# A seven-product form for half of the output projection, spread between HGRN2's last projection tiles, with the residual in four tiles

## The chip, the cores and the metric

The kernel runs on one core of a Trainium2 chip. Its engines work side by side, each on its own queue of instructions: PE (TensorE) multiplies matrices, DVE (VectorE), ACT (ScalarE) and POOL (GpSimd) do elementwise work, and SP issues most of the DMA transfers. The metric is the device time of one execution in microseconds; before the change it is 1578.18 us, the median of three runs.

## The reference, cut to what matters

The block works on 512 tokens of width 1024 in float32: a SwiGLU feed-forward part (FFN1), two token mixers side by side (HGRN2 and Mamba-2), a merge of the two, a second feed-forward part (FFN2), a gate with per-layer embeddings and a last norm. The change lies at the merge:

```
gate_a, gate_b = jnp.split(jax.nn.sigmoid(br_gates), 2, axis=-1)
mixed = gate_a * (o_hg @ w_hg_out[l]) + gate_b * (y @ w_ssm_out[l])
h = h + mixed @ w_out[l]
h = h + 0.5 * swiglu(rms_norm(h, ffn2_norm[l]), ffn2_w13[l], ffn2_w2[l])
```

`w_hg_out` and `w_out` are 1024 x 1024, so `mixed @ w_out` has 512 tokens, an inner dimension of 1024 and 1024 outputs. All products are wanted at float32 accuracy.

## The kernel before

**Three matmuls for one product.** Every operand of a large product is kept as two tiles, a rounded part (hi) and the rest (lo). `split` (L529) makes them: ACT casts (L530), DVE subtracts (L531). `mm` (L515) then issues three matmuls, hi x hi, hi x lo, lo x hi (L518 to L520), into one PSUM bank.

**Units and look-ahead.** The whole kernel is a list of `Unit`s. A unit has weight pieces (`Half`, cut from a `Chunk`) and a function that issues its matmuls. `run` (L388) goes through the list in order. Ahead of each unit it loads and splits weight pieces of later units, as far as the unit's look-ahead numbers allow (`AHEAD`..., L40 to L43) and as `room` (L141) says that enough blocks stay free. After each stretch of matmuls a `slot` lets background work (norms, transposes) advance by a step. What is issued `aside` may be placed elsewhere in its engine's queue by the scheduler behind it, which orders each engine's queue by a modelled timeline when the program is built.

**Memory.** `Arena` holds two blocks of eight units of 1 KB per partition and 46 blocks of four units (`BLOCKS`, L36). `find` (L83) takes the place of least cost: a freed place costs 130 less the number of frees since then, down to 0; tiles of up to four units pay 99 more in a block of eight (L95). `room` counts the empty blocks of four only. A tile of 1024 float32 columns is four units, one whole small block. The residual h (`Tokens`, L284) is two tiles of eight units, with two token tiles of 1024 columns in each; no other tile in the program is that large.

**Seven products.** In both FFNs the matrix products are done two blocks by two in the Strassen-Winograd way, with seven products of half-sized blocks for eight. The order is `ORDER = (1, 2, 6, 5, 7, 3, 4)` (L850), and the names of each product's operands are in `PRODUCTS`: quarters of the weights a, b, d and sums S1 to S4; quarters of the activations e, g, h and sums T1 to T4. A weight chunk of this kind loads five raw pieces, three of which get a second quarter added by a DMA from POOL's queue (`load`, L472); S2 and S4 are summed on DVE (L503, L506). `HiddenQ` (L253) makes the activation operands. The function `down` inside `ffn` (L758) runs the seven products of the FFN's second matrix: each product is 2 x 2 calls of `mm` with 512 columns, and its bank is added straight into two quarters of h by DVE (L780). `_merge` (L1387) spreads two lists of units evenly over one another.

**The stretch around the change.** Gate tiles first; then the eight tiles of `w_hg_out`, each 24 matmuls of 128x512 (`tile`, L659). When tile d is through, `ho_done` (L1526) multiplies its bank with the gate, adds the Mamba-2 share and splits the result: block d of the mixed activations. `mix_end` (L1537) then allocates h, reads it back from DRAM, loads FFN2's norm gain and allocates FFN2's activation operands. `wide` (L824) runs the output projection, one half of the output columns at a time, four token tiles each, 24 matmuls a tile; in the first half the last two inner blocks come in a second pass (`LATE`). `wout_done` (L1567) adds each bank to h on DVE (L1569). After the second half of a token tile its norm starts (`norm_gen`, L572): a square on ACT, a power on POOL, a scaling on DVE (L569), then PE transposes (L208), copies on ACT (L211) and splits. FFN2's first unit `first` (L716) begins with the columns of tokens 0 and 1, 96 matmuls of 128x256, and goes on with those of tokens 2 and 3.

Of the kernel before, what the change touches and what calls it, by code (L numbers as in the profile page):

```python
# [48 lines left out]
FFN_PACE, GATE_PACE = 1, 1.75  # L49
# [3 lines left out]
GATES_FIRST, LATE = 12, 2  # L53
# [10 lines left out]
def _cols(c):  # L64
    return slice(c * P, (c + 1) * P)


class Arena:
# [88 lines left out]
    def free(self, *aps):  # L157
        for ap in aps:
            _, st, lo, k = self.live.pop(id(ap))
            self.clock += 1  # L160
            for i in range(lo, lo + k):
                st[i] = self.clock
# [121 lines left out]
class Tokens:  # L284


    def __init__(self, b):
        self.b = b
        self.half = [b.t(2, D) for _ in range(2)]
        self.c = [self.half[c // 2][:, c % 2, :] for c in range(NC)]  # L290

    def __getitem__(self, c):
        return self.c[c]

    def free(self):
        self.b.fr(*self.half)


class Half:
# [47 lines left out]
class Block:  # L347
# [359 lines left out]
    def ffn(self, h, n, w13, w2, done, then=None):  # L707

        U = self.units
        start = len(U)  # L710
        f0s = [sum(PARTS[:k]) for k in range(len(PARTS) + 1)]
        N = len(PARTS)
        hid = [HiddenQ(self) for _ in PARTS[:-1]] + [Hidden(self, PARTS[-1])]
        v = self.nc.vector
# [40 lines left out]
            v.scalar_tensor_tensor(hd, bank, 0.5, hd, ALU.mult, ALU.add)  # L755
            self.frb(bank)

        def down(k):  # L758


            acc = {}
            ch = Chunk(w2, f0s[k] * P, 4, 0, 2 * 512, "w")

            where = {1: ("A", 1), 2: ("C", 1), 6: ("A", 0), 5: ("B", 1), 7: ("A", 0), 3: ("B", 0), 4: ("A", 0)}
            target = {1: (0, 0), 2: (0, 0), 6: (0, 1), 5: (1, 1), 7: (1, 1), 3: (0, 1), 4: (1, 0)}

            def product(wt, p):
                x, fresh = where[p][0], where[p][1] == 1
                op = hid[k].op.pop(PRODUCTS[p][1])
                ds, th = target[p]  # L770
                if fresh:
                    acc[x] = [self.bank() for _ in range(2)]
                for m in range(2):
                    bank = acc[x][m]
                    for j in range(2):
                        self.mm(bank, tuple(y[:, j, _cols(m)] for y in op), (wt[0][:, j], wt[1][:, j]),
                                fresh and j == 0, j == 1, not fresh)
                    hd = h[0][2 * th + m][:, ds * 512:ds * 512 + 512]
                    with self.aside():
                        v.scalar_tensor_tensor(hd, bank, -0.5 if ds else 0.5, hd, ALU.mult, ALU.add)  # L780
                self.fr(*op)
                if p in (2, 3, 4):
                    self.frb(*acc[x])
                yield FFN_PACE
            return [Unit([next(x for x in ch.halves if x.j == PRODUCTS[p][0])], lambda wt, p=p: product(wt, p)) for p in ORDER]

        def last(*wt, t):

            q = len(wt) // 2
# [20 lines left out]
        for k, size in enumerate(PARTS):  # L810
            x = [u for i in range(0, size, 2) for u in gate_up(k, i)]
            if k:
                U += x[:2] + _merge(x[2:], down(k - 1))
            else:
                U += x
        U.append(Unit([], n_end))
# [3 lines left out]
        U.append(Unit([], lambda: freed(hid[-1])))  # L820
        for u in U[start:]:
            u.ahead = AHEAD_FFN

    def wide(self, act, w, done, late=0):  # L824

# [23 lines left out]
PRODUCTS = {1: ("a", "e"), 2: ("b", "g"), 3: ("S4", "h"), 4: ("d", "T4"), 5: ("S1", "T1"), 6: ("S2", "T2"), 7: ("S3", "T3")}  # L849
ORDER = (1, 2, 6, 5, 7, 3, 4)  # L850


class Seven:
# [8 lines left out]
    def product(self, wt, p, pace):  # L862
        b, st = self.b, self.st
        where = {1: "A", 6: "A", 7: "A", 4: "A", 5: "B", 3: "B", 2: "C"}[p]
        fresh = p in (1, 2, 5)
        if fresh:
            st[where] = b.bank()
        bank = st[where].rearrange("p (j t) -> p j t", j=2)
        wh, wl = wt
        for j in range(2):  # L870
            for k in range(4):
                b.mm(bank[:, j], (wh[:, k, _cols(j)], wl[:, k, _cols(j)]), self.n[0].opk(PRODUCTS[p][1], k),
                     fresh and j == 0 and k == 0, k == 3, j == 1 or not fresh)
        with b.aside():
            self.take(p, bank)
        yield pace
# [529 lines left out]
def _plan(b):  # L1406
    nc, ins = b.nc, b.i
    xr = ins["x"].rearrange("(c p) d -> p c d", p=P)
    hv = b.dram.tile([T, D], F32, name="hscr").rearrange("(c p) d -> p c d", p=P)
    pjv = b.dram.tile([T, D], F32, name="proj").rearrange("(c p) d -> p c d", p=P)  # L1410
    outv = b.out.rearrange("(c p) d -> p c d", p=P)
    U = b.units
    h, n1, n2, n3, n4, mixed, oT = [], [], [], [], [], [], []
# [85 lines left out]
    a, o = hg.plan(1), ssd.plan_out(3)  # L1499
    while a or o:  # L1500
        U.extend(a[:3] + o[:1])
        a, o = a[3:], o[1:]
# [9 lines left out]
    s_, acc = {}, {}  # L1512
# [11 lines left out]
        b.fr(x)  # L1524

    def ho_done(d, bank):  # L1526
        if not mixed:
            mixed.append(Act(b, 0, 1))
            mixed[0].k = [None] * KD
        nc.vector.tensor_tensor(s_[d], s_[d], bank, ALU.mult)  # L1530
        nc.vector.tensor_tensor(s_[d], s_[d], acc[d], ALU.add)
        x = mixed[0].k[d] = b.pair(T)
        mixed[0].blocks.append(x)
        b.split(s_[d], *x)
        b.fr(acc[d], s_[d])

    def mix_end():  # L1537
        oT[0].free()
        h.append(Tokens(b))
        for c in range(NC):  # L1540
            nc.sync.dma_start(h[0][c], hv[:, c, :])
        gains["ffn2"] = b.gain_tile(ins["ffn2_norm"])
        n3.append(ActW(b))
        yield 1
# [6 lines left out]
    gates0 = len(U)  # L1551
    U.append(Unit([], lambda: begin("oT", hg_wait)))
    for w, off, act, done in (("w_in", OFF_GA, n2, ga_done), ("w_in", OFF_GB, n2, gb_done), ("w_hg_out", 0, oT, ho_done)):
        for d in range(0, KD, 2):
            n0 = len(U)
            U.extend(b.tiles(Chunk(ins[w], 0, KD, off + d * P, 256, "c"), act,
                             lambda j, bank, d=d, done=done: done(d + j, bank), GATE_PACE))
            if act is oT and d == 0:
                U[n0].need = ["oT"]
        if done is gb_done:  # L1560
            U.append(Unit([], n2_end))

# [4 lines left out]
    def wout_done(t, dh, acc):  # L1567
        dc = slice(dh * 512, (dh + 1) * 512)
        nc.vector.tensor_tensor(h[0][t][:, dc], h[0][t][:, dc], acc, ALU.add)  # L1569
        if dh == 1:  # L1570
            b.start(("n3", t), b.norm_gen(h[0][t], gains["ffn2"], n3[0], t, wait=1, after=(
                lambda: b.fr(gains["ffn2"])) if t == NC - 1 else None))
            if t == NC - 1:
                mixed[0].free()
    b.wide(mixed, ins["w_out"], wout_done, LATE)


    def done2(t):
# [53 lines left out]
```

## Time and profile before

| what | before |
|---|---|
| median of three runs (lowest to highest) | 1578.18 us (1575.81 to 1579.27) |
| the profiled execution, its span | 1577.02 us, 1575.3 us |
| PE busy | 1537.3 us (98%) |
| DVE busy | 1081.1 us (69%) |
| ACT busy | 754.5 us (48%) |
| POOL busy | 173.3 us (11%) |
| mean DMA rate | 143 GB/s |

The span runs from the first to the last instruction of the profiled execution. A PE that is busy is not a PE at its peak, since neighbouring matmuls overlap and their ends are modelled: the distance between starts says how fast they go.

### The profile page before, as it was taken

The page shows a single profiled execution, that of the slowest core. Times are in us where ns is not written, and L with a number is a line of the kernel's source. Part 1 is how long each engine was busy: PE and PEld are TensorE (multiplying, and loading weights), DVE is VectorE, ACT ScalarE, POOL GpSimd, SP SyncE. Part 2 cuts the span into 40 slices and gives each one's busy share as a digit, 9 for nine tenths or more (in the row PEclk, how much of TensorE's full clock was granted, in tenths as well). Part 3 has the DMA queues.
Part 4 walks back from the last instruction along what each step waited for, and adds up shares of the span by engine and source line. Part 5 has one row for each costly group of instructions (what it writes and reads, how often), then busy time and mean ns, then how long its engine had stood idle before and what let it go on. Part 6 is the DMA issues. An engine that isn't in the chain of part 4 may idle for free.

```text
span 1575.3 us, 22345 instructions
## 1 busy us (share of the span) xinstructions
PE 1537.3 (98%) x8894; PEld 1339.3 (85%) x8894; DVE 1081.1 (69%) x1379; ACT 754.5 (48%) x1093; POOL 173.3 (11%) x230
## 2 busy tenths in 40 slices
PE   8999999999998999999999999999999999999997
PEld 7989999988886887878888788888889999999986
DVE  7789888775568675867646654434348987897853
ACT  6555554554456445452454455433136654545542
POOL 2101101000012010110012011100002011001000
PEclk9999999999999999999999999999999999999999
DMA  9967867565233254364431522342239768676521
GB/s 298 213 160 189 214 147 192 123 208 161 67 95 108 88 167 141 120 182 141 121 100 61 174 69 72 107 134 94 94 90 236 171 175 206 148 193 148 200 68 54
DMA packets 216012, 225.52 MB, mean 143 GB/s; under 512 B 8148, under 2 KB 171748, under 8 KB 215908
## 3 DMA queue, kind: packets, MB, share of 16 engines
q1 hardware_dynamic: 190436, 194.73, 39.9%
q0 software_dynamic: 25472, 29.36, 11.7%
q8 instruction: 70, 1.15, 0.3%
q14 instruction: 34, 0.28, 0.0%
HBM read 209.31 MB, written 14.75 MB: 142 GB/s over the span
## 4 chain that ended last, share of the span: by engine, by line
PE 45%; DMA 5%; DVE 3%; ACT 2%; issue 1%; POOL 1%; DVEq 0%; POOLq 0%; ACTq 0%
PE bank L518 14%; PE bank L519 14%; PE bank L520 14%; DMA blk<-in_ffn_w_dram 4%; DVE blk L531 2%; ACT blk L530 1%; DMA blk<-in_w_in_dram 1%; PE bank L1336 0%; PE bank L1363 0%; PE bank L1331 0%; PE bank L1333 0%; PE bank L1351 0%; PE bank L1110 0%; PE bank L552 0%; PE bank L1365 0%
## 5 line engine op out<-in xcount | busy, mean ns | idle before, releaser
L518 PE MATMUL bank<-blk,blk 128*128 128x512 f32 (+1 forms) x2616 | 900.8, 346 | 17.4 <-ACT blk L530 7.7
L519 PE MATMUL bank<-blk,blk 128*128 128x512 f32 (+1 forms) x2616 | 898.2, 344 | 0.2 <-DVE blk L531 0.2
L520 PE MATMUL bank<-blk,blk 128*128 128x512 f32 (+1 forms) x2616 | 894.0, 344 | 2.5 <-DVE blk L531 2.5
L531 DVE TENSOR_TENSOR blk<-blk,blk 128x1024 fp32r<-128x1024 f32 (+2 forms) x477 | 493.7, 1059 | 206.0 <-ACT blk L530 166.4
L530 ACT CAST blk<-blk 128x1024 fp32r<-128x1024 f32 (+2 forms) x477 | 422.4, 920 | 388.2 <-DMA blk<-in_w_in_dram 79.2
L518 PEld LDWEIGHTS bank<-blk,blk 128*128 128x128 f32 x2616 | 498.0, 191 | 74.6 <-ACT blk L530 9.4
L520 PEld LDWEIGHTS bank<-blk,blk 128*128 128x128 f32 x2616 | 497.1, 191 | 56.0 <-DVE blk L531 2.9
L519 PEld LDWEIGHTS bank<-blk,blk 128*128 128x128 f32 x2616 | 498.8, 191 | 52.9 <-issue 1.0
L482 POOL DMA_DIRECT2D blk<-in_ffn_w_dram x56 | 70.8, 1265 | 484.0 <-DMA blk<-in_ffn_w_dram 384.6
L561 POOL TENSOR_SCALAR small<-small 128x1 f32<-128x1 f32 (+1 forms) x40 | 13.4, 334 | 615.2 <-ACT blk L567 293.6
L780 DVE SCALAR_TENSOR_TENSOR blk<-bank,blk 128x512 f32<-128x512 f32 x112 | 74.7, 682 | 2.3 <-PE bank L520 2.2
L883 ACT COPY blk<-bank 128x512 f32<-128x512 f32 x80 | 46.2, 581 | 45.5 <-PE bank L520 45.4
L995 DVE SCALAR_TENSOR_TENSOR blk<-bank,small,blk 128x511 f32<-128x511 f32 (+2 forms) x72 | 53.6, 744 | 15.1 <-ACT blk L993 14.4
L503 DVE TENSOR_TENSOR blk<-blk,blk 128x1024 f32<-128x1024 f32 x28 | 34.2, 1220 | 37.7 <-DMA blk<-in_ffn_w_dram 37.7
L748 ACT ACTIVATE blk<-blk 128x512 f32<-128x512 f32 x40 | 25.3, 632 | 61.7 <-DVE blk L893 45.8
L1110 PEld LDWEIGHTS bank<-blk,blk 128*128 128x128 f32 x256 | 40.9, 192 | 11.5 <-issue 6.0
L531 DVE TENSOR_TENSOR blk<-bank,blk 128x256 fp32r<-128x256 f32 x68 | 27.0, 418 | 18.8 <-ACT blk L530 18.7
L1110 PE MATMUL bank<-blk,blk 128*128 128x64 f32 x256 | 37.2, 259 | 1.6 <-DVE blk L531 1.6
L993 ACT ACTIVATE blk<-bank,small 128x512 f32<-128x512 f32 x24 | 18.6, 775 | 37.7 <-PE bank L520 37.7
L530 ACT CAST blk<-bank 128x256 fp32r<-128x256 f32 x68 | 23.4, 373 | 25.3 <-PE bank L552 25.1
L1071 DVE TENSOR_TENSOR blk<-blk,blk 128x1024 f32<-128x1024 f32 x16 | 19.6, 1222 | 21.6 <-POOL blk L1069 21.6
L506 DVE TENSOR_TENSOR blk<-blk,blk 128x1024 f32<-128x1024 f32 x28 | 34.1, 1216 | 0.0
(206 smaller groups left out, 1021.0 us busy)
## 6 DMA issues: line engine op xcount, KB each, us to landing
blk<-in_ffn_w_dram SPq DMA_DIRECT2D x160, 512.0 KB, 5.3
blk<-in_w_in_dram SPq DMA_DIRECT2D x89, 512.0 KB, 4.1
blk<-in_ffn_w_dram POOLq DMA_DIRECT2D x56, 512.0 KB, 8.4
blk<-in_w_ssm_out_dram SPq DMA_DIRECT2D x16, 512.0 KB, 4.0
blk<-cscr SPq DMA_DIRECT2D x16, 512.0 KB, 3.9
accscr<-blk SPq DMA_DIRECT2D x32, 256.0 KB, 2.4
blk<-accscr SPq DMA_DIRECT2D x32, 256.0 KB, 2.7
blk<-in_w_hg_out_dram SPq DMA_DIRECT2D x8, 512.0 KB, 4.5
```

What stands on the lines that cost most here:

```text
L482: self.nc.gpsimd.dma_start(c.raw[x], s, accum_op=ALU.add)
L503: v.tensor_tensor(raw["S2"], raw["S1"], raw["S2"], ALU.add)
L506: v.tensor_tensor(raw["S4"], raw["S2"], raw["S4"], ALU.add)
L518: t.matmul(out, lhsT=lh, rhs=rh, start=start, stop=False, skip_group_check=more)
L519: t.matmul(out, lhsT=lh, rhs=rl, start=False, stop=False, skip_group_check=more)
L520: t.matmul(out, lhsT=ll, rhs=rh, start=False, stop=stop, skip_group_check=more)
L530: self.nc.scalar.copy(hi, src)
L531: self.nc.vector.tensor_tensor(lo, src, hi.bitcast(F32), ALU.subtract)
L780: v.scalar_tensor_tensor(hd, bank, -0.5 if ds else 0.5, hd, ALU.mult, ALU.add)
L883: b.nc.scalar.copy(st[p], bank)
L995: nc.vector.scalar_tensor_tensor(t[:, s:], pc[:, 0:T - s], b.cw[:, 3 - s, ct:ct + 1], t[:, s:], ALU.mult, ALU.add)
L1110: nc.tensor.matmul(pyv[:, hh, :], lhsT=R[c][:, hh, :], rhs=xdt[:, hh, :], start=True, stop=True)
```

## The change

The first half of the output projection's inner dimension (blocks 0 to 3 of `mixed`) takes the seven-product form. `down` moves out of `ffn` and becomes a method with the operand holder, the weights, the pace and the scale as arguments; FFN1 and FFN2 call it as before. In `ho_done`, blocks 0 to 3 go into a `HiddenQ`, in two halves of 256 tokens; blocks 4 to 7 stay as they were. After tile 3 a new unit `h_back` allocates h and reads it back. The seven products are merged with tiles 4 to 7, so that the order is product 1, tile 4, products 2 and 6, tile 5, product 5, tile 6, products 7 and 3, tile 7, product 4. The other half of the inner dimension follows `mix_end` as `wout_half`, 12 matmuls for a token tile, without the late pass. h is four tiles of 1024 columns everywhere, in FFN1 too.

```diff
@@ class Tokens
-        self.half = [b.t(2, D) for _ in range(2)]
-        self.c = [self.half[c // 2][:, c % 2, :] for c in range(NC)]
+        self.c = [b.t(D) for _ in range(NC)]
...
@@ ffn
-                U += x[:2] + _merge(x[2:], down(k - 1))
+                U += x[:2] + _merge(x[2:], self.down(h, lambda q=hid[k - 1]: q, w2, f0s[k - 1] * P, FFN_PACE, 0.5))
...
+    def down(self, h, op, w, r0, pace, scale):
...
+        ch = Chunk(w, r0, 4, 0, 2 * 512, "w")
...
+            for m in range(2):
+                bank = acc[x][m]
+                for j in range(2):
+                    self.mm(bank, tuple(y[:, j, _cols(m)] for y in x_op), (wt[0][:, j], wt[1][:, j]),
+                            fresh and j == 0, j == 1, not fresh)
+                hd = h[0][2 * th + m][:, ds * 512:ds * 512 + 512]
+                with self.aside():
+                    v.scalar_tensor_tensor(hd, bank, -scale if ds else scale, hd, ALU.mult, ALU.add)
...
@@ _plan
     def ho_done(d, bank):
-        if not mixed:
+        nc.vector.tensor_tensor(s_[d], s_[d], bank, ALU.mult)
+        if d < 4:
+
+            if d == 0:
+                mixed.append(HiddenQ(b))
+            if d % 2 == 0:
+                o[:] = [b.t(2, T // 2) for _ in range(2)]
+            for th in range(2):
+                ts = slice(th * 256, th * 256 + 256)
+                nc.vector.tensor_tensor(o[th][:, d % 2], s_[d][:, ts], acc[d][:, ts], ALU.add)
+            b.fr(acc[d], s_[d])
+            if d % 2:
+                mixed[0].put(d - 1, list(o))
+            return
+        if d == 4:
             mixed.append(Act(b, 0, 1))
-            mixed[0].k = [None] * KD
-        nc.vector.tensor_tensor(s_[d], s_[d], bank, ALU.mult)
+            mixed[1].k = []
...
+    def h_back():
         h.append(Tokens(b))
         for c in range(NC):
             nc.sync.dma_start(h[0][c], hv[:, c, :])
+        yield 1
+
+    def mix_end():
+        oT[0].free()
...
+        if act is oT:
+            res[0].need = ["oT"]
+            res = res[:4] + [Unit([], h_back)] + _merge(
+                res[4:], b.down(h, lambda: mixed[0], ins["w_out"], 0, GATE_PACE, 1.0))
+        U.extend(res)
...
-    b.wide(mixed, ins["w_out"], wout_done, LATE)
+    for dh in range(2):
+        U.append(Unit(Chunk(ins["w_out"], 512, 4, dh * 512, 512, "k").halves, lambda *wt, dh=dh: wout_half(wt, dh)))
+
+    def wout_half(wt, dh):
+        for t in range(NC):
+            bank = b.bank()
+            b.as_mm(bank, mixed[1], 0, t, wt)
+            wout_done(t, dh, bank)
+            b.frb(bank)
+            yield 1
```

## Rows read from the trace of the kernel before

**Rows 1.** The engine table of the profile's page: busy us (share), instructions.
```profile
PE 1537.3 (98%) x8894; PEld 1339.3 (85%) x8894; DVE 1081.1 (69%) x1379; ACT 754.5 (48%) x1093; POOL 173.3 (11%) x230
```

**Rows 2.** What PE waited for, whole span: total us, times, longest us.
```profile
PE bank L518 <- ACT blk L530: 7.7, 6, 2.2
...
```

**Rows 3.** Windows: length, busy us (instructions) by engine, granted clock, DMA share, GB/s.
```profile
1095.00:1135.00 40.00, 40.00 (x178) 33.15 (x177) 18.77 (x26) 8.47 (x11) 0.00 (x0) 1.00 0.20 65
1135.00:1177.00 42.00, 42.00 (x195) 34.87 (x195) 16.71 (x20) 12.79 (x19) 2.24 (x6) 1.00 0.27 85
1177.00:1225.00 48.00, 45.91 (x381) 45.50 (x380) 42.02 (x53) 29.25 (x46) 8.38 (x8) 1.00 0.97 240
1240.00:1500.00 260.00, 256.80 (x1794) 240.65 (x1793) 215.64 (x259) 131.92 (x174) 26.46 (x21) 1.00 0.70 181
```

**Rows 4.** Timeline of PE: start us, duration us, operation [idle before, releaser].
```profile
1164.28 0.39 PE L518 MATMUL bank<-blk,blk 128*128 128x512 f32 x1
...
1167.00 0.39 PE L518 MATMUL bank<-blk,blk 128*128 128x512 f32 x1
...
1167.46 1.03 PE L208 MATMUL bank<-small,blk 128*128 128x128 f32 x8
...
1176.99 0.28 PE L518 MATMUL bank<-blk,blk 128*128 128x256 f32 x1
...
1192.27 0.91 PE L518 MATMUL bank<-blk,blk 128*128 128x256 f32 x5 [1.87 <-ACT blk L530]
1193.39 0.39 PE L519 MATMUL bank<-blk,blk 128*128 128x256 f32 x1 [0.22 <-DVE blk L531]
```

**Rows 5.** DVE's groups by shape, 1095 to 1240 us: busy us, mean ns | idle.
```profile
L531 DVE TENSOR_TENSOR blk<-blk,blk 128x1024 fp32r<-128x1024 f32 x28 | 33.7, 1219 | 15.0 <-PE bank L520 8.4 <-ACT blk L530 5.6 <-PE bank L519 0.7
...
L531 DVE TENSOR_TENSOR blk<-blk,blk 128x512 fp32r<-128x512 f32 x31 | 20.8, 686 | 8.3 <-ACT blk L530 6.8 <-PE bank L519 1.5
...
L527 DVE SCALAR_TENSOR_TENSOR blk<-blk,blk 128x512 f32<-128x512 f32 x6 | 4.1, 682 | 0.0
...
L503 DVE TENSOR_TENSOR blk<-blk,blk 128x1024 f32<-128x1024 f32 x3 | 3.6, 1216 | 0.0
...
L728 DVE TENSOR_TENSOR blk<-blk,bank 128x256 f32<-128x256 f32 x4 | 1.5, 410 | 0.0
L780 DVE SCALAR_TENSOR_TENSOR blk<-bank,blk 128x512 f32<-128x512 f32 x2 | 1.4, 692 | 0.1
```

**Rows 6.** DMA issues of the page: queue, count, KB each, median us to landing.
```profile
blk<-in_ffn_w_dram SPq DMA_DIRECT2D x160, 512.0 KB, 5.3
...
blk<-in_ffn_w_dram POOLq DMA_DIRECT2D x56, 512.0 KB, 8.4
...
blk<-hscr SPq DMA_DIRECT2D x4, 512.0 KB, 5.1
```

**Rows 7.** Timeline of DVE: the norms of tokens 0 and 1.
```profile
1164.48 0.69 DVE L1569 TENSOR_TENSOR blk<-blk,bank 128x512 f32<-128x512 f32 x1 [1.29 <-PE bank L520]
1167.37 1.28 DVE L569 SCALAR_TENSOR_TENSOR blk<-blk,small,blk 128x1024 f32<-128x1024 f32 x1 [2.20 <-POOL small L562]
1169.72 1.29 DVE L531 TENSOR_TENSOR blk<-blk,blk 128x512 fp32r<-128x512 f32 x2 [1.07 <-ACT blk L530]
...
1174.94 0.69 DVE L531 TENSOR_TENSOR blk<-blk,blk 128x512 fp32r<-128x512 f32 x1
```

**Rows 8.** What SP's DMA queue waited for, 1240 to 1500 us.
```profile
SPq L489 <- DVE blk L531: 135.7, 37, 17.8
...
```

**Rows 9.** Timeline of FFN2: DVE's weight sum and split, PE's product with it.
```profile
1308.09 1.22 DVE L503 TENSOR_TENSOR blk<-blk,blk 128x1024 f32<-128x1024 f32 x1 [7.24 <-DMA blk<-in_ffn_w_dram]
...
1311.57 2.35 DVE L531 TENSOR_TENSOR blk<-blk,blk 128x1024 fp32r<-128x1024 f32 x2
...
1320.98 0.28 PE L518 MATMUL bank<-blk,blk 128*128 128x256 f32 x1
```

**Rows 10.** Timeline of ACT at FFN2's start.
```profile
1188.64 1.57 ACT L530 CAST blk<-blk 128x1024 fp32r<-128x1024 f32 x2 [4.64 <-DMA blk<-in_ffn_w_dram]
...
```

More of the change, by code (lines that the diff above doesn't have):

```diff
@@ L295, in free @@
     def free(self):
-        self.b.fr(*self.half)
+        self.b.fr(*self.c)
 class Half:
@@ L756, in add @@
             self.frb(bank)
[L758 to L785, printed above, removed]
         def last(*wt, t):
@@ L822, in ffn, with product @@
             u.ahead = AHEAD_FFN
+    def down(self, h, op, w, r0, pace, scale):
+        v = self.nc.vector
+        acc = {}
+        ch = Chunk(w, r0, 4, 0, 2 * 512, "w")
+        where = {1: ("A", 1), 2: ("C", 1), 6: ("A", 0), 5: ("B", 1), 7: ("A", 0), 3: ("B", 0), 4: ("A", 0)}
+        target = {1: (0, 0), 2: (0, 0), 6: (0, 1), 5: (1, 1), 7: (1, 1), 3: (0, 1), 4: (1, 0)}
+        def product(wt, p):
+            x, fresh = where[p][0], where[p][1] == 1
+            x_op = op().op.pop(PRODUCTS[p][1])
+            ds, th = target[p]
+            if fresh:
+                acc[x] = [self.bank() for _ in range(2)]
+            for m in range(2):
[6 more added lines that the diff above has]
+                    v.scalar_tensor_tensor(hd, bank, -scale if ds else scale, hd, ALU.mult, ALU.add)
+            self.fr(*x_op)
+            if p in (2, 3, 4):
+                self.frb(*acc[x])
+            yield pace
+        return [Unit([next(x for x in ch.halves if x.j == PRODUCTS[p][0])], lambda wt, p=p: product(wt, p)) for p in ORDER]
     def wide(self, act, w, done, late=0):
@@ L1526, in ho_done @@
     def ho_done(d, bank):
-        if not mixed:
+        nc.vector.tensor_tensor(s_[d], s_[d], bank, ALU.mult)
[12 more added lines that the diff above has]
+        if d == 4:
             mixed.append(Act(b, 0, 1))
-            mixed[0].k = [None] * KD
-        nc.vector.tensor_tensor(s_[d], s_[d], bank, ALU.mult)
+            mixed[1].k = []
         nc.vector.tensor_tensor(s_[d], s_[d], acc[d], ALU.add)
-        x = mixed[0].k[d] = b.pair(T)
-        mixed[0].blocks.append(x)
+        x = b.pair(T)
+        mixed[1].k.append(x)
+        mixed[1].blocks.append(x)
         b.split(s_[d], *x)
         b.fr(acc[d], s_[d])
-    def mix_end():
-        oT[0].free()
+    o = []
+    def h_back():
         h.append(Tokens(b))
@@ L1553, in _plan @@
     for w, off, act, done in (("w_in", OFF_GA, n2, ga_done), ("w_in", OFF_GB, n2, gb_done), ("w_hg_out", 0, oT, ho_done)):
+        res = []
         for d in range(0, KD, 2):
[L1555 to L1559, printed above, removed]
+            res.extend(b.tiles(Chunk(ins[w], 0, KD, off + d * P, 256, "c"), act,
+                               lambda j, bank, d=d, done=done: done(d + j, bank), GATE_PACE))
+        if act is oT:
[3 more added lines that the diff above has]
+        U.extend(res)
         if done is gb_done:
@@ L1573, in wout_done @@
             if t == NC - 1:
-                mixed[0].free()
-    b.wide(mixed, ins["w_out"], wout_done, LATE)
+                mixed[1].free()
+    for dh in range(2):
[7 more added lines that the diff above has]
+            yield 1
     def done2(t):
```

## Prediction

> **What bounds the kernel now.** I read the engine table first [rows 1]: PE is busy in 1537.3 of 1575.3 us. The reader is to see that 38 us of idle time is all that better cover could return; the rest falls only with matmuls. The waits of PE [rows 2] say how it lies: the largest of 14 lines is 7.7 us, in six pieces of 2.2 at most, so no single wait is worth 10. Then the stretches around the change [rows 3]: from 1095 us (HGRN2's output tiles) to 1177 us (the end of the output projection) PE is busy in 82 of 82 us, DVE in 18.77 + 16.71, ACT in 8.47 + 12.79, and the DMA share is 0.20 and 0.27. In the next 48 us, FFN2's start, DVE works 42.02, DMA is at 0.97, and PE loses 2.1. So before 1177 the matmul count sets the time; just behind it the norm, the weight splits and PE are all near their limit.
>
> **The matmuls removed.** The output projection has 4 token tiles x 8 inner blocks x 2 halves x 3 products of `mm` = 192 matmuls of 128x512. The change puts inner blocks 0 to 3 into seven products of 2 x 2 x 3 = 12, 84 in place of 96. Twelve go. Their price is read from starts, not durations: the L518 matmul at 1164.28 and the one twelve matmuls later, at 1167.00, start 2.72 us apart [rows 4], 0.227 each. PE's busy share there is 1.00, so all of it comes off the path: -2.72 us.
> The recorded duration is 0.39 us [rows 4], because neighbours overlap. The Trainium skill's page "Perfetto Trace Analysis" (Identifying the Most-Contended Engine) says that matmul busy time misjudges PE since its instructions are pipelined; the trace agrees (0.39 recorded, 0.227 apart). By durations the gain would be 4.7 us, by starts 2.72.
>
> **What is added on DVE and ACT.** Prices are those of [rows 5]. On DVE: 14 updates of the residual at 0.69 (9.7; the 8 adds of the other half stay as many as before), 11 weight pieces in place of 8 (3 x 1.22 = 3.7), the sums S2 and S4 (2.4), four operand sums (4 x 0.68 = 2.7), 7 operand splits in place of 4 (3 x 0.69 = 2.1), two short adds in place of one in four tiles (4 x 0.13, from the 0.41 of a 256-wide operation = 0.5): 21 us. On ACT three casts of each of two widths, 1.57 for such a pair [rows 10]: 4.7 us. DVE has 46.5 us idle between 1095 and 1177 and ACT 60.7 [rows 3], so I take nothing. If that cover were used up, each further us would be one of PE; I keep +1 us for a single late product, since the operands T1 to T4 (ten operations of 0.7 us on DVE) come in one burst after tile 3 and the product that needs the first sum, the third, runs 2.72 + 5.44 + 2.72 = 10.9 us later.
>
> **DMAs and the queues they pass.** SP issues 9 loads of w_out instead of 8 and POOL 3 adding ones. POOL has nothing else to do before 1161 us (0.00 busy up to 1135) [rows 3]; an adding load lands after 8.4, behind a plain load of 5.3 [rows 6]. The loads come out three to four pieces ahead (the planner's list has some 18 whole blocks free there, counted by following the allocator through the kernel before), over 16 us before the first product; S2 is wanted 10.9 us later still. At the worst the look-ahead shrinks to one tile: the sum S1 lands 5.3 + 8.4 = 13.7 after the issue, S2 needs 1.22 + 1.05 + 1.22 on top, 17.2 in all against 5.44 + 10.9 = 16.3: 0.9 us late. I take zero. The four residual loads (5.1 us each to land [rows 6]) move ahead of those of `w_hg_out`'s last tiles and of w_out's other half in SP's queue; their first reader is the update after product 1, some 3 us after they are issued, and it holds up only the product that writes the same bank again, 8.2 us later. Zero, with the DMA share at 0.20.
>
> **The start of FFN2, where the saving can be lost.** Today each token tile of the last pass takes 24 matmuls, 5.44 us; afterwards 12, 2.72 us. The norms of tokens 0 and 1 must be through before FFN2's first matmul. Call the end of the pass E (1176.99 now [rows 4]). Token 1's add is then at E - 5.1 instead of E - 12.5. From an add to its scaled row takes 4.17 us (1164.48 to 1168.65), from the transposes to their split 3.55 (1167.46 [rows 4] to 1171.01, the end of the two subtractions that begin at 1169.72) [rows 7]: 7.7 at least, so PE waits 2.6 us at E. At the most it is what token 1 took where nobody was in a hurry, 11.15 us (1164.48 to 1175.63) [rows 7]: 6.1 us. Against it stands today's wait for token 3, 1.87 + 0.22 = 2.09 us at 1190 [rows 4]: the second half of `first` now starts later by the first wait, so that most of it goes. Net +0.5 to +4.0 us. I take +1.5, near the lower end, since the compiler orders the queues by need and 7.7 is worked out from rows without a queue ahead.
>
> **The sum.** The profiled execution took 1577.02 us (span 1575.3, 1.7 around it). 1577.02 - 2.72 + 1.5 = 1575.8. The median of the runs is 1578.18, 1.16 above that execution, so the forecast is **1577.0 us**; with the ends of the last term (+0.5, +4.0) and the late product (+1) its own range is 1576 to 1580.5. A measurement of this kernel tells about 0.2% (3.2 us) from no change: this is within it.
>
> **Rivals.**
> (a) *FFN weights come later, slower.* Four residual tiles no longer fit the two blocks of eight units that the pair of halves had to itself; the allocator adds 99 to the cost of a small tile there, so the four go into four of the 46 blocks of four that the weights share, and the two big blocks are hardly used (a freed block costs at most 130). Both FFNs are short of blocks already: SP waits 135.7 us for blocks that DVE's splits give back, 17.8 us at the longest [rows 8], and DVE 7.24 us at 1308.09 for a weight sum still on its way [rows 9]. PE doesn't feel that, as the sum's product starts only at 1320.98 (found by counting products), 7.1 us after the splits that end at 1313.92 [rows 9]. Each product returns about two blocks, so four fewer set a load back by two products of 2.88 us (5.8), inside the 7.1. It decides from a third product (8.6) on, or where DVE's longer wait holds a bank. It can hit the second gate/up piece of four parts in each FFN, eight places: at 1 us each 1577.0 + 8 = 1585, at 1.5 us each 1589. The Trainium skill's page "Perfetto Trace Analysis" (Optimization Strategy) says that the same gap repeating on the engine that should be full can mean too little room for the next tile; today's trace shows no such gap on PE (256.80 of 260 us busy [rows 3]), so by that rule the shortage doesn't bind yet.
> (b) *The whole gain.* The first wait doesn't appear, because weight splits step back behind the norms, and today's 2.09 goes: 1578.18 - 2.72 - 2.09 = 1573.4. For it: in today's 2.09 lies a wait of ACT of 4.64 us for a weight load that stood ahead of token 3's copies [rows 10], a matter of order. Against: the 7.7 us are a chain.
> (c) *The norm chain takes more than the saving.* The first wait is 6.1 us and today's 2.09 stays, since ACT's wait for that load is set by the DMA (share 0.97): 1578.18 - 2.72 + 6.1 = 1581.6. Against: it counts the unhurried chain in full.
> That the change removes fewer matmuls than 12 isn't one: the count is in the code.
>
> **Chances.** Forecast 0.46, (a) 0.29, (b) 0.14, (c) 0.11. Faster by over 0.2% (below 1575.0): (b) and a little of the forecast's low end, 0.15. Slower (above 1581.3): nearly all of (a) and somewhat over half of (c), 0.34. Within: 0.51. The range reaches down to (b) and up into (a) at 1.3 us a place: 1573.3 to 1587.5.
>
> **What would show it.** Twelve matmuls of 128x512 fewer, and PE without a gap from HGRN2's output tiles to E, E some 2.7 us earlier; a gap there means a late operand or weight sum. Behind E, a wait of PE for a split of tokens 0 and 1 of 2.6 us or more, and none or a short one 11.5 us later. In the FFNs, PE's busy time per stretch as before; if (a) holds, new waits of PE on weight splits (L530, L531) recur once per part there, and FFN1, which has no other edit, is longer too. The forecast is wrong if FFN1 alone moves by more than 2 us, or if PE starts FFN2 without a wait.

## The result and the profile after

The changed kernel takes 1606.85 us (median, 1606.05 to 1609.04) beside 1577.59 for the kernel before on the same chip: 1.0176 times as long, 95% interval 1.0155 to 1.0196. The forecast of 1577.0 and its range up to 1587.5 are missed, on the slow side.

In the changed kernel's lines the matmuls are L517 to L519, a split is L529 and L530, the weight sums are L502 and L505, SP's loads L488, POOL's adding loads L481. The engine table, and the largest waits of PE (total us, times, longest):

```profile
PE 1547.4 (96%) x8882; PEld 1343.3 (84%) x8882; DVE 1100.8 (69%) x1409; ACT 762.2 (47%) x1103; POOL 180.6 (11%) x232
```

```profile
PE bank L517 <- ACT blk L529: 16.7, 8, 3.2
PE bank L518 <- DVE blk L530: 6.1, 6, 2.8
...
```

Against [rows 1, 2]: the 12 matmuls are gone (8882), and yet PE is busy 10 us longer; the waits for splits, 7.7 us at the most before, have grown to 16.7 and 6.1. Three DVE rows of the changed kernel say in which stages: the first add of FFN1's last pass, the last add of the output projection, the last add of FFN2.

```profile
364.09 0.69 DVE L754 SCALAR_TENSOR_TENSOR blk<-bank,blk 128x512 f32<-128x512 f32 x1 [2.86 <-PE bank L519]
...
1184.81 0.69 DVE L1590 TENSOR_TENSOR blk<-blk,bank 128x512 f32<-128x512 f32 x1 [0.21 <-PE bank L519]
...
1551.85 0.68 DVE L754 SCALAR_TENSOR_TENSOR blk<-bank,blk 128x512 f32<-128x512 f32 x1
```

The same three of the kernel before:

```profile
349.76 0.69 DVE L755 SCALAR_TENSOR_TENSOR blk<-bank,blk 128x512 f32<-128x512 f32 x1 [2.96 <-PE bank L520]
...
1177.38 0.68 DVE L1569 TENSOR_TENSOR blk<-blk,bank 128x512 f32<-128x512 f32 x1
1521.48 0.69 DVE L755 SCALAR_TENSOR_TENSOR blk<-bank,blk 128x512 f32<-128x512 f32 x1 [1.51 <-PE bank L520]
```

FFN1, which no product of the change touches, ends 14.3 us later. At the end of the output projection 7.4 us of that are left: the mixers and the edited stage gave back 6.9. FFN2 then takes 367.0 us in place of 344.1: 22.9 more. So the loss lies in the two FFNs. (Not all of the 22.9 is loss: with the edit the transposes of tokens 0 and 1 and a wait for them fall behind the output projection and count here, and this length is 352.2 us in e1 below, a kernel as fast as the one before.) Windows of the changed kernel (columns as in [rows 3]): FFN1, the stage of the products, its end, FFN2's start, FFN2.

```profile
60.00:340.00 280.00, 268.00 (x1876) 251.91 (x1876) 227.08 (x274) 141.47 (x185) 30.21 (x24) 0.98 0.68 169
1107.00:1147.00 40.00, 40.00 (x179) 33.10 (x178) 28.95 (x43) 13.65 (x17) 0.00 (x0) 1.00 0.29 85
1147.00:1185.00 38.00, 38.00 (x171) 31.48 (x170) 22.06 (x30) 10.47 (x15) 2.96 (x6) 1.00 0.21 64
1185.00:1233.00 48.00, 42.27 (x327) 40.79 (x326) 38.53 (x51) 29.25 (x47) 8.11 (x9) 0.93 0.86 213
1240.00:1500.00 260.00, 247.32 (x1728) 230.18 (x1728) 215.86 (x260) 130.97 (x173) 27.74 (x22) 0.99 0.66 163
```

And FFN1 of the kernel before:

```profile
60.00:340.00 280.00, 276.38 (x1967) 260.83 (x1966) 238.21 (x284) 147.47 (x193) 31.35 (x25) 0.99 0.71 178
```

The stage of the products is full (78.00 of 78 us), as forecast. In 280 us of FFN1 PE idles 12.0 us in place of 3.6, and the records show 91 matmuls fewer.

**How one gap comes about.** Late in FFN1 of the changed kernel: two rows of SP's DMA queue, one of POOL, four of DVE, one of PE.

```profile
259.49 0.37 SPq L488 DMA_DIRECT2D blk<-in_ffn_w_dram  x1
...
276.15 3.21 SPq L488 DMA_DIRECT2D blk<-in_ffn_w_dram  x4
```

```profile
280.12 1.28 POOL L481 DMA_DIRECT2D blk<-in_ffn_w_dram  x1 [20.30 <-DMA blk<-in_ffn_w_dram]
```

```profile
271.42 1.23 DVE L502 TENSOR_TENSOR blk<-blk,blk 128x1024 f32<-128x1024 f32 x1 [3.46 <-DMA blk<-in_ffn_w_dram]
272.56 3.56 DVE L530 TENSOR_TENSOR blk<-blk,blk 128x1024 fp32r<-128x1024 f32 x4
...
288.20 1.23 DVE L502 TENSOR_TENSOR blk<-blk,blk 128x1024 f32<-128x1024 f32 x1 [5.67 <-DMA blk<-in_ffn_w_dram]
289.34 2.35 DVE L530 TENSOR_TENSOR blk<-blk,blk 128x1024 fp32r<-128x1024 f32 x2
```

```profile
290.61 0.50 PE L518 MATMUL bank<-blk,blk 128*128 128x512 f32 x1 [1.94 <-DVE blk L530]
```

SP issues no weight load for 16.3 us after 259.86, since the next one wants a block that is still being read. At 276.15, during the four splits that begin at 272.56, it goes on; POOL adds at 280.12; DVE waits 5.67 us for that landing; the splits follow, and PE has waited 1.94 us for one. From the load to PE it is 14.5 us: the loads no longer run ahead of that. Who held the block is in SP's waits from 255 to 296 us:

```profile
SPq L488 <- DVE blk L530: 17.5, 2, 16.2
...
SPq L488 <- PE bank L519: 1.6, 1, 1.6
```

The long wait ends with a split on DVE, which had itself waited for a load (3.46 us at 271.42), and not with PE. So this gap shows how late loads reach PE; why the loads of this kernel came to be late is not in it.

### The profile page after: what moved, and what is told of

The parts are those of the page before. It is cut to its first block, busy times and chain, and to the rows that moved or that the text cites. A ratio compares the mean times of both kernels' runs of the same rounds, so it can differ in the third digit from the quotient of the medians.

```text
span 1604.9 us, 22375 instructions
## 1 busy us (share of the span) xinstructions
PE 1547.4 (96%) x8882; PEld 1343.3 (84%) x8882; DVE 1100.8 (69%) x1409; ACT 762.2 (47%) x1103; POOL 180.6 (11%) x232
## 4 chain that ended last, share of the span: by engine, by line
PE 77%; DMA 11%; DVE 6%; issue 2%; ACT 2%; POOL 1%; SPq 0%; DVEq 0%; POOLq 0%; ACTq 0%
PE bank L517 23%; PE bank L518 23%; PE bank L519 23%; DMA blk<-in_ffn_w_dram 8%; DVE blk L530 4%; PE bank L1110 1%; ACT blk L529 1%; DMA blk<-in_w_in_dram 1%; PE bank L551 1%; DMA blk<-cscr 1%; PE bank L1108 1%; DMA proj<-blk 1%; PE bank L1104 1%; DMA blk<-in_x_dram 1%; DVE blk L817 1%
## 5 line engine op out<-in xcount | busy, mean ns | idle before, releaser
L517 PE MATMUL bank<-blk,blk 128*128 128x512 f32 (+1 forms) x2607 | 900.9, 348 | 26.6 <-ACT blk L529 16.7
L519 PE MATMUL bank<-blk,blk 128*128 128x512 f32 (+1 forms) x2607 | 892.1, 344 | 2.8 <-DVE blk L530 2.8
L529 ACT CAST blk<-blk 128x1024 fp32r<-128x1024 f32 (+2 forms) x483 | 428.4, 921 | 465.4 <-PE bank L518 101.0
L530 DVE TENSOR_TENSOR blk<-blk,blk 128x1024 fp32r<-128x1024 f32 (+2 forms) x483 | 499.7, 1060 | 198.2 <-ACT blk L529 182.6
L517 PEld LDWEIGHTS bank<-blk,blk 128*128 128x128 f32 x2607 | 499.8, 192 | 87.3 <-ACT blk L529 19.8
L519 PEld LDWEIGHTS bank<-blk,blk 128*128 128x128 f32 x2607 | 498.6, 192 | 55.4 <-DVE blk L530 3.8
L481 POOL DMA_DIRECT2D blk<-in_ffn_w_dram x56 | 70.7, 1263 | 505.6 <-DMA blk<-in_ffn_w_dram 233.5
L502 DVE TENSOR_TENSOR blk<-blk,blk 128x1024 f32<-128x1024 f32 x29 | 35.5, 1224 | 74.9 <-DMA blk<-in_ffn_w_dram 74.9
L817 DVE SCALAR_TENSOR_TENSOR blk<-bank,blk 128x512 f32<-128x512 f32 x126 | 84.9, 683 | 0.2 <-PE bank L519 0.2
L995 DVE SCALAR_TENSOR_TENSOR blk<-bank,small,blk 128x511 f32<-128x511 f32 (+2 forms) x72 | 53.5, 743 | 15.1 <-ACT blk L993 14.3
L530 DVE TENSOR_TENSOR blk<-bank,blk 128x256 fp32r<-128x256 f32 x68 | 25.9, 418 | 23.1 <-ACT blk L529 23.1
L529 ACT CAST blk<-bank 128x256 fp32r<-128x256 f32 x68 | 22.4, 378 | 32.0 <-PE bank L551 31.7
L505 DVE TENSOR_TENSOR blk<-blk,blk 128x1024 f32<-128x1024 f32 x29 | 35.3, 1218 | 0.0
L1069 POOL TENSOR_SCALAR_AFFINE_SELECT blk<-blk 128x1024 f32<-128x1024 f32 x16 | 20.8, 1303 | 117.7 <-DMA blk<-cscr 96.0
L561 POOL TENSOR_TENSOR small<-small 128x1 f32<-128x1 f32 (+1 forms) x40 | 32.1, 803 | 3.2
```

The source lines that it names most:

```text
L481: self.nc.gpsimd.dma_start(c.raw[x], s, accum_op=ALU.add)
L502: v.tensor_tensor(raw["S2"], raw["S1"], raw["S2"], ALU.add)
L505: v.tensor_tensor(raw["S4"], raw["S2"], raw["S4"], ALU.add)
L517: t.matmul(out, lhsT=lh, rhs=rh, start=start, stop=False, skip_group_check=more)
L519: t.matmul(out, lhsT=ll, rhs=rh, start=False, stop=stop, skip_group_check=more)
L529: self.nc.scalar.copy(hi, src)
```

## The experiments

Two numbers say where a loss lies: when FFN1 ends and how long FFN2 takes, both by the DVE rows above, each of a single execution. Each ratio compares with the kernel before on the same chip, whose median there was 1577.6 to 1579.5 us. The last column is counted by following the allocator through each program: of the 70 loads of raw weight pieces that FFN1 (and FFN2) makes for its seven-product chunks, how many of the last 55 take a block that last held *split* weights, which PE reads. Most others take a block that last held raw weights, which a split reads (39 in the kernel before, 27 in the changed one); up to ten take one of split activations, which PE reads too (9 and 5).

| kernel | median us | ratio to before, 95% | FFN1 ends | FFN2 takes | loads into split weights' blocks |
|---|---|---|---|---|---|
| before | 1577.59 | | 349.8 | 344.1 | 6, 6 |
| changed | 1606.85 | 1.0155 to 1.0196 | 364.1 | 367.0 | 19, 20 |
| e1 changed, 50 blocks of four | 1577.25 | 0.9982 to 1.0007 | 349.2 | 352.2 | 6, 6 |
| e2 before, four tiles | 1619.83 | 1.0233 to 1.0285 | 365.2 | 375.6 | 19, 22 |
| e3 before, four tiles, 50 blocks | 1576.69 | 0.9971 to 1.0000 | 349.0 | 343.6 | 6, 6 |
| e4 changed, halves in FFN1 | 1618.23 | 1.0229 to 1.0274 | 349.1 | 388.9 | 6, 22 |
| e5 changed, one half in FFN1 | 1611.07 | 1.0191 to 1.0241 | 348.2 | 373.2 | 9, 20 |
| e6 50 blocks, token order | 1577.65 | 0.9979 to 1.0004 | 351.9 | 345.9 | 6, 6 |
| e7 changed, no toll | 1604.86 | 1.0148 to 1.0190 | 362.7 | 353.5 | 8, 9 |
| e8 changed, 5 to spare | 1612.01 | 1.0180 to 1.0239 | 366.0 | 364.6 | 24, 25 |
| e9 50 blocks, 1 to spare | 1578.46 | 0.9972 to 1.0005 | 353.6 | 348.2 | 5, 5 |
| e10 50 blocks, late splits | 1578.62 | 0.9978 to 1.0013 | 356.9 | 345.0 | 6, 6 |
| e11 changed, type 15 | 1587.85 | 1.0040 to 1.0086 | 355.8 | 356.9 | 6, 7 |
| e12 50 blocks, type 0 | 1613.98 | 1.0203 to 1.0251 | 369.0 | 365.9 | 30, 30 |
| e13 50 blocks, type 15 | 1590.95 | 1.0063 to 1.0104 | 355.6 | 357.5 | 0, 0 |
| e14 50 blocks, type 15 late | 1577.39 | 0.9981 to 1.0009 | 351.8 | 347.7 | 1, 1 |
| e15 changed, type 15 late | 1582.90 | 1.0015 to 1.0048 | 349.9 | 355.7 | 9, 10 |
| e16 before, type 15 late | 1577.35 | 0.9981 to 1.0008 | 355.0 | 341.8 | 1, 1 |

**Memory or products (e1 to e3).**

```diff
-BLOCKS = [8] * 2 + [4] * 46
+BLOCKS = [4] * 50
```

> The changed kernel with its memory cut into 50 blocks of four units in place of 2 of eight and 46 of four: the residual's four tiles then leave 46 blocks to the weights, as before the change. Theory M (the two blocks of eight stand nearly unused, weights come late in both FFNs): FFN1 ends again near 350 us instead of 364.1, FFN2 loses its part of +22.9, the time is 1574 to 1581 us, what is left above or below 1577.6 being the 12 matmuls and FFN2's start. Theory R1 (the seven products of the output projection, their loads and sums cost it): FFN1 may come back, but the time stays near 1595 or above. Theory R2 (any edit reshuffles the queues by some tens of us): no definite value, FFN1 not back at 350.

> The kernel before with one edit: the residual in four tiles of 1024 columns, blocks as they were (2 of eight, 46 of four). Theory M: all of the loss in the FFNs, without the seven products: FFN1 ends near 364, the time is 1595 to 1608 us. Theory R1: FFN1 and the time as before, 1576 to 1580. Theory R2: slower or not, but with PE's waits in other places than in the changed kernel.

 (Its edit is the diff of `Tokens` alone.)

> The kernel before with the residual in four tiles and 50 blocks of four: the same memory as in the changed kernel with 50 blocks, without the seven products. Theory M: 1576 to 1580 us, FFN1 ends near 350; its distance to the changed kernel with 50 blocks is what the seven products are worth by themselves: by the prediction's terms -2.72 + (0.5 to 4.0), that is -2.2 to +1.3 us. Theory R1: 1576 to 1580 as well, but the changed kernel with 50 blocks 15 us or more above it. Theory R2: above 1585.

With 50 blocks of four the whole loss is gone (e1); the four tiles without the products lose even more than the change, and more than expected (e2), and with 50 blocks nothing (e3). So the four tiles together with the two blocks of eight cost the 29 us, and the seven products by themselves can't be told from nothing: 1577.25 beside 1576.69.

In e1 the stage of the products can be read undisturbed. From the first product of `ho_done` to the last pair of `Silu`s of FFN2's `first` it takes 108.80 us, in e3 110.04: 1.24 less. PE behind the pass in e1:

```profile
1172.37 1.09 PE L208 MATMUL bank<-small,blk 128*128 128x128 f32 x8 [0.23 <-DVE blk L568]
1176.62 1.07 PE L208 MATMUL bank<-small,blk 128*128 128x128 f32 x8 [3.15 <-ACT blk L529]
...
1179.54 0.39 PE L518 MATMUL bank<-blk,blk 128*128 128x256 f32 x1 [1.26 <-DVE blk L530]
```

and in e3, where it is PE's only wait there:

```profile
1189.07 0.58 PE L517 MATMUL bank<-blk,blk 128*128 128x256 f32 x2 [1.96 <-ACT blk L529]
```

**Which FFN, how many blocks (e4, e5).** `Tokens` has its two halves in FFN1 (e4), or one half and two tiles of 1024 columns (e5), and four tiles in FFN2:

```diff
-        self.c = [b.t(D) for _ in range(NC)]
+        self.own = [b.t(2, D), b.t(D), b.t(D)]      # e5, FFN1 only
+        self.c = [self.own[0][:, 0, :], self.own[0][:, 1, :]] + self.own[1:]
```

> The changed kernel, with FFN1's residual in two tiles of eight units as before the change and FFN2's in four tiles. Theory M (room for weights in the FFN itself): FFN1 ends near 349.5 us in place of 364.1, FFN2 keeps its loss, the time is 1606.9 - 14.6 = 1592 us (1588 to 1596). Theory R2 (queues reshuffled by any edit, over the whole program): FFN2's length changes as well, by several us.

> The changed kernel, with FFN1's residual as one tile of eight units and two of four: one block of eight is used, one stands empty, two blocks of four go instead of four. FFN2 as in the changed kernel. Theory M with a price per block: FFN1 ends near 357 us, time near 1599. Theory M with a slack that the first two blocks use up (the prediction's reckoning: a set-back by one product, 2.9 us, inside 7.1): FFN1 ends at 349.5 to 352, time near 1593. If it doesn't matter how many blocks but only that the residual's tiles are small: FFN1 at 364, time 1607.

FFN1 came out as expected in both: no loss with the halves, none with two blocks fewer (348.2). The times did not. FFN2, whose tiles are the changed kernel's, lost 22 us more in e4 and 6 more in e5, and in e5 the mixers, from the end of FFN1 to the first product of `ho_done`, took 752.7 us instead of 744.0. A likely reason, not tested, is that what the allocator left behind in FFN1 decides where FFN2's tiles lie; the loss there has no fixed size for four blocks. A version with one block of eight and 48 of four, meant to halve the loss of room, finds no place for one of its tiles, so it has no time.

**FFN2's start (e6).** e1 with the rest of the output projection token by token:

```diff
-    for dh in range(2):
-        U.append(Unit(Chunk(ins["w_out"], 512, 4, dh * 512, 512, "k").halves, ...))
+    for t in range(NC):
+        U.append(Unit(wo[0] + wo[1], lambda *wt, t=t: wout_rest(wt, t)))
```

> The changed kernel with 50 blocks of four and one edit more: the other half of the output projection goes token by token, both halves of the output columns one behind the other, with both weight halves loaded ahead; so token 1's last add is 10.9 us before the end of the pass in place of 5.4. Theory S (the gain of 12 matmuls is handed back at FFN2's start by the norm chain of tokens 0 and 1): PE's waits of 3.15, 0.23 and 1.26 us behind the pass go, at most a wait of 2 us for token 3 comes back: 1577.3 - (2 to 4.6) = 1572.6 to 1575.3 us. Rival: the start is set by when FFN2's first weights are there, not by the norms: no change, 1576 to 1578.

1577.65: no gain that can be measured. Theory S was right that the three waits are the norms' and go with the other order: PE has no gap behind the pass in e6. But one comes back 20 us later, before the columns of tokens 2 and 3:

```profile
1193.52 0.58 PE L517 MATMUL bank<-blk,blk 128*128 128x256 f32 x1 [3.71 <-ACT blk L529]
```

It is 3.71 us where 2 at most were expected, with the granted clock at 0.94 over 1180 to 1240: moved, not saved.

**The toll and the order of loads (e7 to e10).**

> The changed kernel with its blocks as they are (2 of eight, 46 of four), but without the 99 that a tile of up to four units pays in a block of eight. Theory M with the toll as the cause: weights and operands move into the two blocks of eight, FFN1 ends at 349 to 352, time 1575 to 1583. If the look-ahead test, which counts empty blocks of four only, is what keeps the loads back: FFN1 stays at 358 to 364, time 1595 to 1607.

(e7: `+ 99 * (k <= 4 < len(st))` left out.) FFN2 came back (353.5), FFN1 did not (362.7), and the mixers took 753.9 us (741.8 in the changed kernel): the toll alone isn't it.

```diff
-AHEAD_FFN = (6, 10, 16, 1, 3, 3)
+AHEAD_FFN = (6, 10, 16, 1, 3, 5)      # e8
+AHEAD_FFN = (6, 10, 16, 1, 1, 1)      # e9, 50 blocks
+AHEAD_FFN = (6, 10, 16, 1, 6, 3)      # e10, 50 blocks
```

> The changed kernel, blocks as they are; in the FFNs a raw weight load must now leave 5 empty blocks of four instead of 3, so that the whole set of five pieces is loaded later, but into blocks given back at least four frees earlier (in the changed kernel one set per FFN begins in the block given back last; mean age 6.4 frees there, 7.7 before the change, 9.5 here). How far ahead the splits stand (8.97 in the changed kernel, 9.72 before, 9.03 here) and how many blocks change their number type (68, 46, 70) stays as in the changed kernel. Theory L (a load waits for a block whose last reader is a split that itself waits for a load): FFN1 ends at 349 to 352, time below 1585. Theory P (splits stand fewer products ahead): FFN1 stays at 360 to 366, time 1600 to 1610. Theory K (a block that changes its type waits for all its readers): the same as P.

> The changed kernel with 50 blocks of four, and weight loads and splits in the FFNs may leave a single empty block instead of 3: they are placed further ahead (9.95 in place of 9.72), types change as seldom (44), but 7 of the 55 raw loads of FFN1 take a block given back at most one free ago. Theory L: both FFNs get longer, FFN1 ends at 358 or later, time 1595 or more. Theory P: no loss or a gain, FFN1 at 347 to 350, time 1573 to 1578. Theory K: no loss, 1575 to 1580.

> The changed kernel with 50 blocks of four, and splits further than six units ahead must leave 6 empty blocks instead of 3: the splits stand 7.95 units ahead on average, at the least 6, less than in the changed kernel (8.97, at the least 6), while no raw load takes a block younger than two frees and types change 40 times. Theory L: no loss, FFN1 ends at 348 to 352, time 1575 to 1582. Theory P: a loss at least like that of the changed kernel, FFN1 at 360 or later, time 1600 or more. Theory K: no loss.

L falls: without young blocks the loss stays (e8), with seven of them it doesn't come (e9). P falls too: splits placed later than in the changed kernel cost FFN1 7.6 us and the whole nothing measurable (e10). Theory K, on blocks that change their type, fitted all three. Of its changes one kind stood out in the count: raw loads in blocks of split weights, 24 in e8, 5 and 6 in e9 and e10.

**Where the loads land (e11 to e13).** `find` adds `pack` for a block of the other number type; it is 4 in the FFNs. (`pack` also weighs half of the units that a tile leaves free in its block, so the edits move that term as well. Room doesn't show it: at a raw load of FFN1 8.3 blocks of four are empty on average in e1, 8.2 in e12, 8.0 in e13; 6.9 in the changed kernel, 6.8 in e11 and e15, counted by following the allocator.)

```diff
-            u.ahead = AHEAD_FFN
+            u.ahead, u.pack = AHEAD_FFN, 15      # e11; e13 with 50 blocks; e12: 0, 50 blocks
```

> The changed kernel, blocks as they are, and one number changed in both FFNs: a tile pays 15 in place of 4 when it takes a block that last held the other number type (raw weights are f32, split weights fp32r). Room stays as short as in the changed kernel (splits stand 9.07 units ahead on average, 8.97 there, 9.72 before), but of the 55 raw loads of FFN1 only 6 take a block of split weights, which PE must have read before (19 in the changed kernel, 6 before the change); 49 take a block that a split has read. Theory K2 (what costs is that raw loads wait for PE to be through with a product's weights): both FFNs as before, FFN1 ends at 348 to 353, time 1574 to 1583. Theory P2 (what costs is the room itself, wherever the loads land): FFN1 at 360 to 366, time 1598 to 1610.

> The changed kernel with 50 blocks of four, and in both FFNs a tile pays nothing for taking a block of the other number type: room as ample as before the change (splits 9.72 units ahead, no load into a block younger than three frees), but 30 of the 55 raw loads of FFN1 take a block of split weights. Theory K2: a loss at least like that of the changed kernel, FFN1 ends at 362 or later, time 1600 or more. Theory P2: no loss, FFN1 at 349 to 352, 1575 to 1580.

> The changed kernel with 50 blocks of four and 15 for the other number type in both FFNs: ample room, and no raw load takes a block of split weights (0 of 55; 6 before the change). Theory K2: the last waits of this kind go too; the FFNs of the kernel before have some 3 us of idle PE each, so 1572 to 1577. Theory P2: no change against 50 blocks alone, 1576 to 1579.

e12 decides between K2 and P2: ample room and 30 such loads give back the loss, 1613.98. e11 is the counterpart, the same shortage with 6 such loads: 19 of the 29 us return, fewer than K2 expected (1574 to 1583). Waits between 60 and 340 us in e12 (total us, times, longest):

```profile
SPq L488 <- DVE blk L530: 157.0, 17, 25.3
SPq L488 <- PE bank L519: 90.5, 17, 18.3
...
DVE blk L502 <- DMA blk<-in_ffn_w_dram: 12.3, 5, 3.3
...
ACT blk L529 <- DMA blk<-in_ffn_w_dram: 45.2, 10, 9.2
```

in e11:

```profile
SPq L488 <- DVE blk L530: 212.0, 56, 13.5
SPq L488 <- PE bank L519: 28.6, 7, 6.4
...
DVE blk L502 <- DMA blk<-in_ffn_w_dram: 26.1, 6, 9.1
...
ACT blk L529 <- DMA blk<-in_ffn_w_dram: 6.0, 3, 3.7
```

in the changed kernel:

```profile
SPq L488 <- DVE blk L530: 152.1, 30, 22.1
SPq L488 <- PE bank L519: 73.2, 15, 14.6
...
DVE blk L502 <- DMA blk<-in_ffn_w_dram: 36.0, 9, 7.3
...
ACT blk L529 <- DMA blk<-in_ffn_w_dram: 32.4, 10, 5.9
```

and in the kernel before:

```profile
SPq L489 <- DVE blk L531: 135.6, 36, 17.7
SPq L489 <- PE bank L520: 61.2, 13, 17.2
...
DVE blk L503 <- DMA blk<-in_ffn_w_dram: 16.5, 6, 6.5
...
ACT blk L530 <- DMA blk<-in_ffn_w_dram: 8.9, 4, 5.5
```

SP's waits for PE are 28.6 us (e11) and 61.2 (before) with 6 such loads, 73.2 with 19, 90.5 with 30. They prove little by themselves: SP waits some 250 of these 280 us in all four, only the shares differ, and in e8, with 24 such loads and as slow as the changed kernel, the waits for PE are 67.9 us. What DVE and ACT then wait for landings goes better with the loss: 25 us before, 68 after, 58 in e12, 32 in e11.

e13 missed: K2 gave it a gain, and it lost 13 us. In FFN1 both 15s lose at the beginning only, as e11's windows show:

```profile
60.00:120.00 60.00, 49.45 (x330) 46.26 (x329) 40.88 (x49) 26.56 (x35) 6.34 (x5) 0.89 0.59 142
120.00:180.00 60.00, 60.00 (x426) 56.54 (x425) 55.08 (x67) 33.05 (x43) 7.51 (x6) 1.00 0.78 195
```

From 120 to 340 us PE doesn't idle, with the shortage still there; the loss is at FFN1's beginning, while the blocks still have the types of what came before. In FFN2 e13 has one such gap, 10.69 us at 1228.50, and e11 waits of 2.59 and 1.19 us at 1307 as well.

**The same, only later (e14 to e16).** 15 from the third of five parts on:

```diff
+            if k == 2:
+                late = len(U)
...
+        for u in U[late:]:
+            u.pack = 15
```

> The changed kernel with 50 blocks of four, and 15 for the other number type only from the third of the five parts of each FFN on (one raw load of 55 in a block of split weights). With 15 from the start, PE lost 7.7 us between 60 and 120 us and nothing from 120 to 340 (60.00 of 60 busy in each stretch). Theory K2: the loss at the start goes and the gain later stays: FFN1 ends at 346 to 350 us, time 1570 to 1576. Rival (the loss between 60 and 120 only moves to where the 15 begins): 1583 to 1592.

> The changed kernel, blocks as they are, with 15 for the other number type from the third part of each FFN on (9 raw loads of 55 in blocks of split weights, 19 without it). Theory K2: most of the loss goes, FFN1 ends at 350 to 356, time 1578 to 1588. Theory P2 (the room itself): 1598 or more.

> The kernel before with the same 15 from the third part of each FFN on. Theory K2: as for the changed kernel with 50 blocks, the waits left in the later parts (some 4 us in both FFNs together) go: 1573 to 1577 beside 1578. Rival (loss where the 15 begins): 1583 to 1592.

e15, the changed kernel with its blocks untouched, is back at 1582.90: 24 of the 29 us, FFN1's loss entirely (349.9). The 13 us of e13 don't come when the number begins later (e14). Neither e14 nor e16 is faster than before, though K2 gave both a gain: the six loads of the kernel before cost nothing that this number can win back. Whether they cost nothing is open, since the number has a price of its own: in e16 PE waits 2.86 us at 162.46, where the kernel before has no wait, and FFN1 ends 5.2 us later. No version beats the kernel before by more than can be measured; the lowest is e3.

## Why the prediction was wrong, step by step

**The matmuls** were right: twelve fewer, no gap from the output tiles to E. **The work on DVE and ACT, the loads and their order** were right at zero: 78.00 of 78 us. (POOL gets two adding loads for w_out, not three: `load` adds a second quarter to S1 and S3 alone, and the page of the changed kernel lists 2. The term stays nothing.)

**FFN2's start** lay inside its range where the FFN doesn't disturb it, but above the value taken. The first wait is 3.15 + 0.23 + 1.26 = 4.6 us in e1, inside 2.6 to 6.1, and the second, 1.96 us in e3, is gone: +2.7 us, where +1.5 was taken and +0.5 to +4.0 allowed. That uses up the 2.72 us of the twelve matmuls, and the times agree: e1 and e3 can't be told apart. That the stage is 1.24 us shorter in e1 by its rows on DVE and ACT, and -2.72 + 1.5 says 1.22, is luck: both ends hang on the queues of these engines, and two single executions don't settle a difference of that size.

In the changed kernel itself the same stretch takes 116.72 us, 7.9 more than in e1. There a weight cast stands on ACT in front of token 0's square and waits for its load, and another one later in front of `Silu`'s table load:

```profile
1178.23 1.05 ACT L529 CAST blk<-blk 128x1024 fp32r<-128x1024 f32 x1 [9.30 <-DMA blk<-in_ffn_w_dram]
1179.18 1.05 ACT L566 ACTIVATE blk<-blk 128x1024 f32<-128x1024 f32 x1
...
1213.53 1.05 ACT L529 CAST blk<-blk 128x1024 fp32r<-128x1024 f32 x1 [6.99 <-DMA blk<-in_ffn_w_dram]
```

PE's waits behind E are

```profile
1189.93 1.06 PE L208 MATMUL bank<-small,blk 128*128 128x128 f32 x8 [2.10 <-ACT blk L529]
1192.80 2.05 PE L517 MATMUL bank<-blk,blk 128*128 128x256 f32 x6 [1.81 <-ACT blk L529]
```

and two short ones, 4.5 us in all, no more than e1's 4.6. What comes on top is a lower granted clock (last section) and ACT's lateness, since the stretch ends with a row of ACT behind the second cast; how the 7.9 us divide between the two was not worked out.

**The step that failed** stands in rival (a), and by it the forecast took the FFNs at nothing: "Each product returns about two blocks, so four fewer set a load back by two products of 2.88 us (5.8), inside the 7.1." It counted blocks as alike. The mechanism of (a), late FFN weights from four blocks fewer, is what happened, and FFN1 moved by 14.3 us where more than 2 was named as the sign against the forecast; but it was priced at 8 us, and what it reckoned with isn't what costs. Two blocks fewer cost FFN1 nothing (e5). Four fewer leave `find` too few blocks of the raw type in the middle of an FFN, so that 19 raw loads instead of 6 fall into blocks of split weights, at a price of 4 for the other type. These landings without the shortage cost all (e12); the shortage without most of them leaves 5 of the 29 us in e15 and 10 in e11, of which e13 puts a part down to the number itself. So it is the type of the blocks that was left out of the reckoning. Why the type costs time is argued, not shown: a load into a block of split weights can be issued only when PE has finished that product, while a block of raw weights is free as soon as a split, which runs products ahead, has read it, and the loads behind it on SP's queue wait too. The one gap followed above hung on a split.

The Trainium skill's page "Perfetto Trace Analysis" (Optimization Strategy) says that the same gap repeating on the engine that should be full can mean too little room. The prediction noted that today's trace had no such gap. The changed kernel has gaps (12.0 us of 280 in FFN1) and too little room, and more blocks, as in e1, take them away: there the sign was true. In e12 the same stretch loses more, 17.1 us, four gaps of 2.6 to 5.7 us among them, with the room of e1:

```profile
60.00:340.00 280.00, 262.86 (x1867) 247.91 (x1866) 224.51 (x267) 138.76 (x181) 30.11 (x24) 0.98 0.65 157
```

So the number of blocks is not the whole of it; their type decides as well.

**Open.** K2, the raw loads alone, was not separated from K, all changes of type: the tiles of split weights that take a block of the raw type, over the whole of FFN1, rise and fall with the loads (34 before, 46 in the changed kernel, 67 in e12, 19 in e11, 26 in e15, counted by following the allocator). In e7 FFN1 loses 13 us with 8 such loads; there small tiles shared the blocks of eight, and nothing was run to separate that. FFN2 lost from 15 to 37 us over e1 at 20 to 22 such loads (the changed kernel, e2, e4, e5): the count doesn't give the size. Why the 15 costs 13 us at an FFN's beginning was not followed further.

## What to carry to other kernels

Before counting whether a smaller pool still feeds the busiest engine, ask for each reused buffer what it held and who reads it last: here the same 50 blocks cost nothing (e1) or 36 us (e12), by which of them the loads landed in. A change of shape in one tile (here the residual) can strand memory that nothing else fits, and the price is paid in stages that the change doesn't name; an untouched stage that moves, as FFN1 here, is the first place to look.

## What the hardware showed beside this

A gap of PE can cost more than its length. Windows of the changed kernel: in the first PE is busy 15.65 of 20 us, and in the next the granted clock is 0.91, the mean over a stretch at the lower of the two levels (1.2 GHz) and the rest at 2.4; behind E it is 0.83.

```profile
260.00:280.00 20.00, 15.65 (x115) 14.63 (x114) 16.45 (x24) 9.67 (x14) 0.00 (x0) 1.00 0.66 141
280.00:300.00 20.00, 17.82 (x123) 17.05 (x124) 12.77 (x14) 7.48 (x10) 2.56 (x2) 0.91 0.58 128
...
1190.00:1210.00 20.00, 17.85 (x126) 17.02 (x127) 17.68 (x27) 11.70 (x21) 2.61 (x3) 0.83 0.63 162
```

At the lower level matmuls of 128x256 start 0.21 us apart (1195.54 to 1195.76), at the higher 0.12 (1200.03 to 1200.15). The mean over the span is 0.989, before the change 0.994: by that some 16 us more at the lower level, and some 7 us more for the same matmuls, an estimate from these figures. It explains a part of why PE is busy 10 us longer with 12 matmuls fewer, and the sum of PE's waits understates the loss.
